# One of four gated one-hots built by two ScalarE activations instead of one VectorE instruction

## The chip, the cores and the metric

The kernel runs as one program on one core of a Trainium2 chip. A core has a matrix engine (TensorE, "PE" in the profile, with its weight loads as "PEld"), three engines for elementwise work (VectorE "DVE", ScalarE "ACT", GpSimd "POOL") and a queue engine that issues most transfers (SyncE "SP"). The metric is the device time of one execution in microseconds (us). Every engine takes its own instructions in a fixed order and waits at semaphores for the others.

## The reference, cut to what matters

The reference is a two-block transformer on 512 tokens of width 1024. The change lies in its last part, a mixture with 16,384 experts whose index is a pair (ia, ib) of 128 by 128:

```python
def _peer(h, w_q, sub_keys_1, sub_keys_2, expert_u, expert_v):
    ...
    best, ci = lax.top_k(cand, PEER_TOPK)
    ia = jnp.take_along_axis(i1, ci // PEER_TOPK, axis=-1)
    ib = jnp.take_along_axis(i2, ci % PEER_TOPK, axis=-1)
    expert_idx = ia * PEER_NKEYS + ib
    gates = jax.nn.softmax(best, axis=-1)
    ...
        a = jax.nn.gelu(jnp.einsum('td,thkd->thk', hx, u).astype(jnp.float32), approximate=False) * gx
        return jnp.einsum('thk,thkd->td', a.astype(hx.dtype), v)
```

Each token chooses 8 heads x 16 = 128 experts, each with a gate. Gates are softmax values, so they are not negative.

## The kernel before, in words

For 384 of the 512 tokens the kernel does not gather the chosen experts. It computes the activation of all experts for all 384 tokens, and multiplies by a dense table of gates that is zero where an expert was not chosen. (The other 128 tokens gather their experts' rows later.) This makes three stages of `phase_c` (line 1008 on):

1. Scores, top-16 choices, and 19 blocks of expert activations ahead (`pull(8 * 19)`).
2. **The gate stage**, which the change touches (lines 1087 to 1130). A column of 128 partitions holds the 128 choices of one token. For each token, `o1` is the one-hot of `ia` along 128 columns, `o2` is the one-hot of `ib` times the gate, and one product of the two sums the 128 choices into the token's 128 x 128 table of gates. Four tokens make a group, 384 tokens make 96 groups, 8 groups make a chunk `c` of 32 tokens, and there are 12 chunks.
3. The weighted sum over experts: per block `j` of 128 experts the table times the activations, then three matmuls per output tile (lines 1254 to 1256).

`T` holds the transposed `ia`, `ib` and gate of 128 tokens (line 1099, a ScalarE copy out of PSUM), so that one token's value is one column, a number for each partition. `one_hots(g)` makes the operands of group `g`: one VectorE comparison of 512 columns for `o1` (line 1107), and for `o2` four instructions of 128 columns (line 1112), `iota == ib` times gate: three on VectorE, and `u = 3` on GpSimd. `o1` and `o2` have three buffers each, so the one-hots of a group can be written when the matmuls of the third group before it have read theirs.

TensorE's order is written by hand: the four products of group `g` (line 1125, each is recorded as two matmuls), then one step of the next expert block (`pull(1)`, line 1081, three matmuls at lines 85 to 87). Eight steps make a block: its weights `wr` come by a SyncE transfer, ScalarE rounds them into `wh` (line 79, 128 x 1024), GpSimd takes the remainder `wl` (line 81), and after the eighth step ScalarE applies Gelu into `a` (line 1036). After each group ScalarE copies the 512 columns of the product from PSUM into `gb` with a stride (line 1128), and after each chunk it issues the transfer of `gb` to memory (line 1130). VectorE, ScalarE, GpSimd and SyncE have their orders from a scheduler in this stage; instructions wait in that order.

After the last group 16 further steps stand on TensorE, and the first `w`, `wh` and `wl` of stage 3 are made; SyncE loads the gate table back (`G`) and the first expert rows (`vr`).

Of the kernel before, what the change touches and what calls it, by code (L numbers as in the profile page):

```python
# [9 lines left out]
F32 = mybir.dt.float32  # L10
# [3 lines left out]
AF = mybir.ActivationFunctionType  # L14
# [11 lines left out]
TD = 384  # L26
NE = 16384
NA = 28
POOL_U = (3,)
POOL_A = True  # L30
LAG = 20
ZB, RT = (0, 1, 7), (1.5, 1.1)
# [13 lines left out]
class Build:  # L46
# [538 lines left out]
    def phase_b(self):  # L585
# [16 lines left out]
        with tc.tile_pool(name="pg", bufs=1, reuse_waits="tile") as pg:  # L602
# [134 lines left out]
            def decays(h):  # L737
                q, k = qk[2 * h], qk[2 * h + 1]
                T = 1.0 / 16
                b6, b12 = self.s2(name="b64"), self.s2(name="b128")  # L740
# [7 lines left out]
                dec = pg.tile([128, 4], F32, name="dec", tag="dec", bufs=2)  # L748
                for t, src, sc, by, e in ((qd, b6, T, q, nc.vector), (ki, b6, -T, k, nc.vector),
                                          (k2, d12, T, k, nc.gpsimd), (ke, d6, T, k, nc.gpsimd),  # L750
                                          (q2, b12, T, q, nc.vector)):
                    nc.scalar.activation(t, src, AF.Exp, scale=sc)
# [255 lines left out]
    def phase_c(self, x3):  # L1008
        nc, i, tc, pc = self.nc, self.i, self.tc, self.pc
# [6 lines left out]
        iota = pc.tile([128, 128], F32, name="iota")  # L1016
# [22 lines left out]
        with tc.tile_pool(name="p1", bufs=1, reuse_waits="tile") as p1:  # L1039
# [22 lines left out]
            for tt in range(4):  # L1062
                t = p1.tile([128, 1024], F32, name="x3t", tag="S_", bufs=3)
                for hf in range(2):
                    ps = self.bank()
# [19 lines left out]
        def pull(n):  # L1085
            for _ in range(n):
                next(al, None)
                self.pulled += 1

        with tc.tile_pool(name="p2", bufs=1, reuse_waits="tile") as p2:  # L1090
            ia, ib, gt = self.choose(0, NT, vals, idxs, p2)
            pull(8 * 19)
            Ts = []
            for tt in range(NT):
                ps = self.bank()
                for n, t in enumerate((ia, ib, gt)):
                    nc.tensor.transpose(ps[:, 128 * n:128 * n + 128], t[:, tt], self.ident)
                T = p2.tile([128, 3, 128], F32, name="T", tag="T", bufs=3)
                nc.scalar.activation(T, ps[:, :384].rearrange("p (n t) -> p n t", t=128), AF.Copy)
                Ts.append(T)  # L1100

            def one_hots(g):

                T, t0 = Ts[g // 32], 4 * (g % 32)
                o1 = p2.tile([128, 4, 128], F32, name="o1", tag="o1", bufs=3)
                o2 = p2.tile([128, 4, 128], F32, name="o2", tag="o2", bufs=3)
                nc.vector.tensor_tensor(o1, iota[:, None, :].to_broadcast([128, 4, 128]),
                                        T[:, 0, t0:t0 + 4].unsqueeze(2).to_broadcast([128, 4, 128]),
                                        op=OP.is_equal)
                for u in range(4):  # L1110
                    e = nc.gpsimd if u in POOL_U else nc.vector
                    e.tensor_scalar(o2[:, u], iota, T[:, 1, t0 + u:t0 + u + 1], T[:, 2, t0 + u:t0 + u + 1],
                                    op0=OP.is_equal, op1=OP.mult)
                return o1, o2

            oh = {0: one_hots(0)}
            for c in range(TD // 32):
                gb = self.xp.tile([128, 128, 32], F32, name="gb", tag="X")
                for g in range(8 * c, 8 * c + 8):
                    if g + 1 < TD // 4:  # L1120
                        oh[g + 1] = one_hots(g + 1)
                    o1, o2 = oh.pop(g)
                    ps = self.bank()
                    for u in range(4):
                        nc.tensor.matmul(ps[:, 128 * u:128 * u + 128], o1[:, u], o2[:, u], start=True, stop=True)
                    pull(1)
                    gs = 4 * (g % 8)
                    nc.scalar.activation(gb[:, :, gs:gs + 4].rearrange("p j t -> p t j"),
                                         ps.rearrange("p (t j) -> p t j", j=128), AF.Copy)
                nc.scalar.dma_start(out=gd[c], in_=gb)  # L1130
            spx = self.xp.tile([128, 4, 1024], F32, name="spx", tag="X")
            h2t, ysp, rep, fg = [spx[:, n] for n in range(4)]

            n = TD // 32 - 1
            G = {0: spx[:, 2:].rearrange("p n d -> p (n d)")[:, :4 * TD].rearrange("p (c t) -> p c t", t=128)}
            nc.sync.dma_start(out=G[0][:, :n], in_=gd[:n, :, :4].rearrange("c p j t -> p c (j t)"))
            nc.scalar.activation(G[0][:, n], gb[:, :4].rearrange("p j t -> p (j t)"), AF.Copy)
            pull(8)
# [3 lines left out]
        for hf in range(2):  # L1142
            ps = self.bank()
# [6 lines left out]
        with tc.tile_pool(name="p3", bufs=1, reuse_waits="tile") as p3:  # L1150
# [88 lines left out]
            for j in range(NJ):  # L1239
# [34 lines left out]
                if j == last + 2:  # L1274
                    assert es == 256 and not got
                    for hf in range(2):
                        ps = self.bank()
# [193 lines left out]
```

## Time and profile before

| what | value |
|---|---|
| median of 3 runs | 2256.93 us (2253.89 to 2257.43) |
| the profiled execution | 2257.13 us, of which the span is 2255.3 us |
| PE busy | 2131.9 us, 95% |
| DVE, ACT, POOL busy | 75%, 42%, 38% |
| gate stage, first group to last copy | 1098.3 to 1252.2 us |

The span runs from the first to the last recorded instruction; 1.8 us of the execution lie outside it. A share of busy time is a mean over stages with different limits, so the rows further below are taken from the gate stage and from the places where the same kinds of instruction occur elsewhere.

### The profile page before, as it was taken

To read this page: it belongs to the slowest core of one execution; us is meant where nothing else is said; L and a number is where in the kernel's file an instruction comes from. 1 tells how busy PE (TensorE), PEld (TensorE's weight loads), DVE (VectorE), ACT (ScalarE), POOL (GpSimd) and SP (SyncE) were. 2 spreads that over 40 slices of the span, in tenths; PEclk is the share of its full clock that TensorE was granted. 3 is DMA by queue.
4 is the path that set the end of the run, shared out by engine and by line. 5 is a ranking of instruction groups with operands and counts; after the bars stand their busy time and mean duration, and the time that the engine had idled before them with its cause. 6 is when DMAs were issued, how large, how long until landed. Compare 5 with 4: busy or idle time off the path is not lost. (4 is left out here: it accounts for less than half of the span.)

```text
span 2255.3 us, 31436 instructions
## 1 busy us (share of the span) xinstructions
PE 2131.9 (95%) x11443; PEld 1877.8 (83%) x11443; DVE 1692.6 (75%) x3304; ACT 958.5 (42%) x1429; POOL 847.9 (38%) x630
## 2 busy tenths in 40 slices
PE   8999999989999999999699889999999999999996
PEld 5778988877888889899688878888888888888875
DVE  6877348996667555879999678777777787877875
ACT  5376446344245533343477433333333333333332
POOL 4333330110056313335699224444444444444200
PEclk9999999999999999999899999999999999999998
DMA  6511223214822132233254659899899898899952
GB/s 249 182 48 63 79 82 112 90 57 132 274 89 66 66 107 91 93 124 120 99 202 197 227 177 333 303 322 319 307 320 312 293 319 308 309 312 309 336 184 74
DMA packets 163164, 433.08 MB, mean 192 GB/s; under 512 B 13248, under 2 KB 69952, under 8 KB 161472
## 3 DMA queue, kind: packets, MB, share of 16 engines
q1 hardware_dynamic: 121536, 267.47, 35.2%
q0 software_dynamic: 36864, 134.23, 17.2%
q10 hardware_dynamic: 4608, 29.36, 3.3%
q8 instruction: 90, 1.47, 0.3%
q14 instruction: 66, 0.54, 0.1%
HBM read 399.56 MB, written 31.46 MB: 191 GB/s over the span
## 5 line engine op out<-in xcount | busy, mean ns | idle before, releaser
L79 ACT ACTIVATE wh<-wr 128x1024 fp32r<-128x1024 f32 (+2 forms) x278 | 291.3, 1048 | 608.9 <-issue 341.0
L85 PE MATMUL bank<-h2h,wh 128*128 128x384 f32 (+2 forms) x1176 | 417.3, 355 | 22.3 <-ACT a L1036 17.5
L87 PE MATMUL bank<-h2h,wl 128*128 128x384 f32 (+2 forms) x1176 | 400.9, 341 | 4.4 <-POOL wl L81 4.4
L86 PE MATMUL bank<-h2l,wh 128*128 128x384 f32 (+2 forms) x1176 | 400.2, 340 | 0.0
L81 POOL TENSOR_TENSOR wl<-wr,wh 128x1024 fp32r<-128x1024 f32 (+2 forms) x89 | 213.9, 2407 | 414.2 <-ACT wh L79 412.0
L1255 PE MATMUL bank<-wl,wwh 128*128 128x512 f32 x768 | 302.8, 394 | 2.5 <-DVE wl L81 2.5
L1254 PE MATMUL bank<-wh,wwh 128*128 128x512 f32 x768 | 300.5, 391 | 2.3 <-ACT wwh L79 2.3
L1256 PE MATMUL bank<-wh,wwl 128*128 128x512 f32 x768 | 302.3, 394 | 0.0
L1159 POOL DMA_INDIRECT rows<-in_u_rows,sidx x128 | 176.8, 1381 | 292.4 <-DVE junk L1166 186.1
L81 DVE TENSOR_TENSOR wl<-wr,wh 128x1024 fp32r<-128x1024 f32 x189 | 233.4, 1236 | 50.5 <-ACT wh L79 49.4
L1159 POOL DMA_INDIRECT rows<-in_v,sidx x128 | 178.4, 1394 | 245.2 <-DVE spx L1176 206.0
L85 PEld LDWEIGHTS bank<-h2h,wh 128*128 128x128 f32 x1176 | 224.3, 191 | 51.8 <-ACT a L1036 43.7
L87 PEld LDWEIGHTS bank<-h2h,wl 128*128 128x128 f32 x1176 | 223.7, 190 | 9.4 <-POOL wl L81 5.3
L86 PEld LDWEIGHTS bank<-h2l,wh 128*128 128x128 f32 x1176 | 224.5, 191 | 4.9
L81 DVE TENSOR_TENSOR wwl<-w,wwh 128x384 fp32r<-128x384 f32 x128 | 71.5, 559 | 162.5 <-ACT wwh L79 162.5
L1255 PEld LDWEIGHTS bank<-wl,wwh 128*128 128x128 f32 x768 | 145.1, 189 | 32.3 <-DVE wl L81 3.7
L1254 PEld LDWEIGHTS bank<-wh,wwh 128*128 128x128 f32 x768 | 145.2, 189 | 31.1 <-ACT wwh L79 2.7
L1256 PEld LDWEIGHTS bank<-wh,wwl 128*128 128x128 f32 x768 | 145.2, 189 | 30.5
L1176 DVE SCALAR_TENSOR_TENSOR spx<-rows,coef,spx 128x1024 f32<-128x1024 f32 x127 | 162.9, 1282 | 2.5
L81 DVE TENSOR_TENSOR wl<-vr,wh 128x1024 fp32r<-128x1024 f32 x112 | 137.1, 1224 | 35.5 <-ACT wh L79 35.5
L85 PE MATMUL bank<-hh,wh 128*128 128x512 f32 (+1 forms) x408 | 160.6, 394 | 1.2 <-ACT rel L626 0.7
L1166 DVE SCALAR_TENSOR_TENSOR junk<-rows,spx 128x1024 bf16<-128x1024 f32 x128 | 156.5, 1223 | 2.8
(433 smaller groups left out, 4573.2 us busy)
## 6 DMA issues: line engine op xcount, KB each, us to landing
wr<-in_u SPq DMA_DIRECT2D x128, 512.0 KB, 5.8
vr<-in_v SPq DMA_DIRECT2D x112, 512.0 KB, 5.1
wada<-in_w_adaT SPq DMA_DIRECT2D x48, 512.0 KB, 4.3
wr<-in_w_b SPq DMA_DIRECT2D x48, 512.0 KB, 3.5
gates_d<-gb ACTq DMA_DIRECT2D x12, 2048.0 KB, 6.9
G<-gates_d SPq DMA_DIRECT2D x31, 768.0 KB, 9.5
wr<-in_w_q SPq DMA_DIRECT2D x16, 512.0 KB, 3.5
wr<-in_v SPq DMA_DIRECT2D x16, 512.0 KB, 5.3
```

The lines of the kernel that those rows point to most:

```text
L79: nc.scalar.activation(hi, src, AF.Copy)
L81: e.tensor_tensor(lo, src, hi.bitcast(F32), op=OP.subtract)
L85: mm(ps, wh, ah, start=first, stop=False)
L86: mm(ps, wh, al, start=False, stop=False)
L87: mm(ps, wl, ah, start=False, stop=last)
L1159: nc.gpsimd.indirect_dma_start(out=r, out_offset=None, in_=table, in_offset=bass.IndirectOffsetOnAxis(ap=ix, axis=0))
L1166: nc.vector.scalar_tensor_tensor(junk, r, 1.0, h2t, op0=OP.mult, op1=OP.mult, accum_out=asp[:, e:e + 1])
L1176: nc.vector.scalar_tensor_tensor(ysp, r, coef[:, e:e + 1], ysp, op0=OP.mult, op1=OP.add)
L1254: nc.tensor.matmul(y, wh[:, ts_], vh[:, ns], start=(jj == 0), stop=False)
L1255: nc.tensor.matmul(y, wh[:, ts_], vl[:, ns], start=False, stop=False)
L1256: nc.tensor.matmul(y, wl[:, ts_], vh[:, ns], start=False, stop=(jj == NJ - 1))
```

## The change

`T` gets a fourth column block, the negated gate, by one more ScalarE copy for each of the three `T`. In `one_hots`, token `u = 1` of a group is no longer made by VectorE but by ScalarE in two steps: the square of `ib - iota`, and then the positive part of `gate - gate * square` in place. The square is 0 at the chosen column and at least 1 elsewhere, so the result is the gate at that column and 0 elsewhere. The second step waits for the first by a semaphore of ScalarE itself.

```diff
-POOL_U = (3,)
+POOL_U, ACT_U = (3,), (1,)
...
-                T = p2.tile([128, 3, 128], F32, name="T", tag="T", bufs=3)
-                nc.scalar.activation(T, ps[:, :384].rearrange("p (n t) -> p n t", t=128), AF.Copy)
+                T = p2.tile([128, 4, 128], F32, name="T", tag="T", bufs=3)
+                nc.scalar.activation(T[:, :3], ps[:, :384].rearrange("p (n t) -> p n t", t=128), AF.Copy)
+                nc.scalar.activation(T[:, 3], ps[:, 256:384], AF.Copy, scale=-1.0)
...
                 for u in range(4):
+                    if u in ACT_U:
+
+                        ib, gate, minus = [T[:, n, t0 + u:t0 + u + 1] for n in (1, 2, 3)]
+                        nc.scalar.activation(o2[:, u], iota, AF.Square, bias=ib, scale=-1.0)
+                        nc.scalar.activation(o2[:, u], o2[:, u], AF.Relu, bias=gate, scale=minus)
+                        continue
                     e = nc.gpsimd if u in POOL_U else nc.vector
```

The new lines shift the numbers: the copy into `gb` is line 1135 in the changed kernel, its transfer 1137, the square 1115 and the positive part 1116.

On ScalarE, before, a chunk in the middle of the gate stage is eight copies into `gb`, one rounding `wh`, one Gelu `a` and one transfer:

```order
L1128 ACTIVATE gb_10728<-bank_10736 128x4x128
L1128 ACTIVATE gb_10728<-bank_10755 128x4x128
L1128 ACTIVATE gb_10728<-bank_10771 128x4x128
L1128 ACTIVATE gb_10728<-bank_10793 128x4x128
L1128 ACTIVATE gb_10728<-bank_10809 128x4x128
L1128 ACTIVATE gb_10728<-bank_10825 128x4x128
L1128 ACTIVATE gb_10728<-bank_10841 128x4x128
L79 ACTIVATE wh_10920<-wr_10918 128x1024
L1128 ACTIVATE gb_10728<-bank_10857 128x4x128
L1036 ACTIVATE a_10880<-bank_10743 128x384
L1130 DMA gates_d_8407<-gb_10728 128x4096
```

Now each copy has a square and a positive part beside it; this is the middle of the same chunk:

```order
L1115 ACTIVATE o2_10787<-iota_8411,T_10429 128x128
L1115 ACTIVATE o2_10810<-iota_8411,T_10429 128x128
L1116 ACTIVATE o2_10787<-o2_10787,T_10429 128x128
L1116 ACTIVATE o2_10810<-o2_10810,T_10429 128x128
L1135 ACTIVATE gb_10748<-bank_10794 128x4x128
L1115 ACTIVATE o2_10827<-iota_8411,T_10429 128x128
L79 ACTIVATE wh_10951<-wr_10949 128x1024
L1116 ACTIVATE o2_10827<-o2_10827,T_10429 128x128
L1135 ACTIVATE gb_10748<-bank_10817 128x4x128
L1115 ACTIVATE o2_10844<-iota_8411,T_10429 128x128
L1116 ACTIVATE o2_10844<-o2_10844,T_10429 128x128
L1135 ACTIVATE gb_10748<-bank_10834 128x4x128
```

In the stage's 96 groups there are now 288 instructions for what were 96; in 48 groups the positive part stands right behind the square that it waits for, as in the last group shown, and in 48 another instruction stands between. The number of activation-table loads in the whole program is 32 in both kernels.

On SyncE, at the end of the gate stage, this is the order before (`spx` takes the first gates, `vr` the first expert rows of stage 3, `wr` the weights of a further block):

```order
L1136 DMA spx<-gates_d 128x11x128
L1196 DMA vr<-in_v 128x1024 x2
L91 DMA wr<-in_u 128x1024
L1184 DMA G<-gates_d 128x12x128 x2
L1196 DMA vr<-in_v 128x1024 x2
```

And now:

```order
L1143 DMA spx<-gates_d 128x11x128
L91 DMA wr<-in_u 128x1024
L1203 DMA vr<-in_v 128x1024 x2
L1191 DMA G<-gates_d 128x12x128 x2
L1203 DMA vr<-in_v 128x1024 x2
```

The two loads of `vr` have moved behind the load of `wr`. TensorE's order is the same in both.

## Rows read from the trace of the kernel before

**Rows 1.** Busy time by engine in the gate stage (windows: us, then engines, clock, DMA)
```profile
1097.00:1110.00 13.00, 12.71 (x81) 12.31 (x80) 12.70 (x37) 8.23 (x11) 12.42 (x9) 0.79 0.00 0
...
1098.50:1252.30 153.80, 141.26 (x1061) 138.41 (x1062) 151.71 (x382) 114.57 (x119) 150.79 (x106) 0.99 0.51 194
...
1150.00:1170.00 20.00, 17.07 (x132) 16.50 (x131) 20.00 (x48) 13.70 (x14) 20.00 (x14) 1.00 0.62 237
```
**Rows 2.** Groups by form, 1097 to 1252 us: busy us, mean ns, idle before
```profile
L1112 DVE TENSOR_SCALAR o<-iota,T 128x128 f32<-128x128 f32 x288 | 107.9, 428 | 0.0
...
L1128 ACT ACTIVATE gb<-bank 128x512 f32<-128x512 f32 x96 | 103.3, 1095 | 39.2 <-PE bank L1125 38.0
...
L79 ACT ACTIVATE wh<-wr 128x1024 fp32r<-128x1024 f32 x11 | 11.7, 1066 | 0.0
L1036 ACT ACTIVATE a<-bank 128x384 f32<-128x384 f32 x11 | 5.9, 533 | 0.0
```
**Rows 3.** Waits in the gate stage: total us, times, longest
```profile
ACT gb L1128 <- PE bank L1125: 38.0, 67, 2.3
...
PE bank L1125 <- DVE o L1112: 10.2, 8, 1.7
```
**Rows 4.** Timeline of PE, two groups that follow each other: start, us, instruction
```profile
1182.06 1.05 PE L1125 MATMUL bank<-o,o 128*128 128x128 f32 x8
...
1183.48 0.72 PE L1125 MATMUL bank<-o,o 128*128 128x128 f32 x5
```
**Rows 5.** Timeline of POOL, DVE and PE around one stall
```profile
1189.06 2.87 POOL L81 TENSOR_TENSOR wl<-wr,wh 128x1024 fp32r<-128x1024 f32 x1
...
1189.62 2.90 DVE L1112 TENSOR_SCALAR o<-iota,T 128x128 f32<-128x128 f32 x3
...
1193.04 0.92 DVE L1112 TENSOR_SCALAR o<-iota,T 128x128 f32<-128x128 f32 x3
...
1192.15 1.15 PE L1125 MATMUL bank<-o,o 128*128 128x128 f32 x8 [1.43 <-DVE o L1112]
```
**Rows 6.** Timeline of ACT where it does not wait
```profile
1185.45 1.06 ACT L79 ACTIVATE wh<-wr 128x1024 fp32r<-128x1024 f32 x1
1186.40 1.09 ACT L1128 ACTIVATE gb<-bank 128x512 f32<-128x512 f32 x1
1187.27 0.54 ACT L1036 ACTIVATE a<-bank 128x384 f32<-128x384 f32 x1
...
1187.95 2.02 ACT L1128 ACTIVATE gb<-bank 128x512 f32<-128x512 f32 x2
```
**Rows 7.** Groups of ACT by form, whole span
```profile
L537 ACT ACTIVATE hh<-tmp,ada 128x256 fp32r<-128x256 f32 x16 | 7.0, 498 | 7.6 <-DVE tmp L535 7.6
...
L496 ACT ACTIVATE qb<-x,fe 128x256 f32<-128x256 f32 x6 | 3.0, 508 | 7.0 <-DVE x L494 4.1 <-DVE hl L538 1.6 <-POOL qb L138 1.3
...
L497 ACT ACTIVATE qa<-x 128x256 f32<-128x256 f32 x6 | 2.4, 401 | 0.0
...
L1137 ACT ACTIVATE spx<-gb 128x128 f32<-128x128 f32 x1 | 0.3, 300 | 0.0
```
**Rows 8.** Timeline of ACT, an activation that reads the one before it
```profile
395.61 0.62 ACT L752 ACTIVATE q<-b 128x512 f32<-128x512 f32 x1
396.26 0.21 ACT L754 ACTIVATE dec<-q 128x4 f32<-128x4 f32 x1
```
**Rows 9.** Timeline of ACT, first groups of the stage
```profile
1100.41 1.09 ACT L1128 ACTIVATE gb<-bank 128x512 f32<-128x512 f32 x1 [1.49 <-PE bank L1125]
1102.88 1.09 ACT L1128 ACTIVATE gb<-bank 128x512 f32<-128x512 f32 x1 [1.38 <-PE bank L1125]
```
**Rows 10.** Timeline of SP and ACT at the end of the stage
```profile
1246.44 1.16 SPq L1196 DMA_DIRECT2D vr<-in_v  x2
1255.58 0.33 SPq L91 DMA_DIRECT2D wr<-in_u  x1
...
1258.82 2.00 ACT L79 ACTIVATE wh<-vr 128x1024 fp32r<-128x1024 f32 x2
```

## The prediction

> **What bounds the kernel now.** The change touches only the gate stage, so I read that stage and not the page's shares. First the busy time by engine in the stage's 153.8 us [rows 1]: DVE and POOL are recorded as busy nearly all of it, PE for 141.3 and ACT for 114.6. That looks like a stage bound by VectorE, with ScalarE having room. The reader is to check this look in two ways.
>
> The first is the pace of PE. Two undisturbed groups start 1.42 us apart (1182.06 and 1183.48) [rows 4], and no wait of PE falls there. So between stalls PE is the bound: 96 groups at 1.42 us are 136.3 us. The rest of the stage, 17.5 us, is the slow start and a stall of about 1.5 us in eight chunks. In such a stall [rows 5] POOL does a remainder `wl` of 2.87 us, DVE's three one-hots take 2.90 us instead of 0.92, and PE then sits idle for 1.43 us until DVE's `o` comes; there are 8 such waits, 10.2 us together [rows 3]. This is all that a faster VectorE can give back.
>
> The second is what ScalarE really has free. The sum of recorded durations misleads, because neighbours overlap in the records. Where ACT does not wait [rows 6], a copy into `gb` begins at 1186.40 and the next instruction at 1187.27: it holds the engine for about 0.88 us, not the 1.09 recorded. A `wh` holds it 0.95 us (1185.45 to 1186.40), and Gelu with the transfer issue behind it 0.68 (1187.27 to 1187.95). By the counts in [rows 2] ScalarE holds 96 x 0.88 + 11 x 0.95 + 11 x 0.68 = 84.5 + 10.5 + 7.5 = 102.5 us of the stage's 153.8. So 51 us are free, most of it as waits for PE's product (38.0 us, 67 times [rows 3]). Per group that is 0.53 us.
>
> **What the change removes.** On VectorE 96 of 288 instructions of 128 columns; three take 0.92 us [rows 5], so a group loses 0.31 us. VectorE then has slack before PE, and with three buffers the stall of [rows 5] is mostly covered. On its own this would be worth up to the stalls.
>
> **What it adds on ScalarE.** 96 squares and 96 positive parts. No such instruction with 128 columns and these operands stands in the trace of before, so I build it from neighbours. A plain 128-column activation from SBUF to SBUF takes 300 ns [rows 7]. An operand that is a column of numbers costs about 0.1 us: 256 columns with a column as scale 508 ns, with a column as bias 498, with neither 401 [rows 7]. So a square (bias a column) records 0.395 us. The positive part has two columns, bias and scale; the second may cost nothing (0.395) or the same again (0.49). I take 0.49, since a column costs the same in either place and there is no row in which one is free. Neighbours that don't depend on each other overlap by 0.1 us (`wh`, 1.06 long, and its successor 0.95 later [rows 6]); an activation that reads the one before starts 0.03 us after its end (395.61 + 0.62, then 396.26 [rows 8]). So:
>
> - a square with something else behind it: 0.30 us, 48 of them: 14.4
> - a square with its own positive part right behind it, which waits for its end: 0.425 us, 48 of them: 20.4
> - a positive part: 0.395 us (0.30 if the second column is free), 96 of them: 37.9 (28.8)
>
> Together 72.7 us (63.6) against 51.3 free. ScalarE becomes the bound, and the stage grows by 72.7 - 51.3 = 21.4 us (12.3). If ScalarE had no such self-wait and a free second column, 96 x 0.60 = 57.6 would leave +6.3; if no neighbour overlapped, 96 x (0.395 + 0.49) + 1.5 for the self-waits = 86.5 would make it +35.2. These are the ends of the range for this term.
>
> The Trainium skill, "ScalarE: Activation LUTs", section "What ACT_TABLE_LOAD costs", gives an activation 186 ns plus 0.833 ns per column, about 93 ns more for each pointer operand, and 93 ns of overlap. The rows agree to a few ns for none and one pointer (293 against 300 ns, +93 against +97 and +107); no row has two. By that rule the positive part holds the engine 0.39 us and the stage grows by 20 us; by a free second operand it would be 12.3.
>
> Does ScalarE keep busy, or does it also wait? In its new order a group's one-hot is made about two copies ahead of that group's own copy, so PE has some 2 us to follow before ScalarE asks for its product. What stands behind a waiting positive part is the next copy, `wh` for GpSimd and PE, Gelu and the gate transfer; all become later together, so nothing beyond the stage's own growth is charged. The negated gates, three small copies, fall in part into the gaps between the `T` copies: 0.4 us. At the start PE is granted 0.79 on average, so part of the stretch to 1110 us is at the lower level of 1.2 GHz [rows 1]; the first two copies are 2.47 us apart, each after a wait of 1.4 us [rows 9]; there ScalarE can't work at its own pace, about 1 us more.
>
> **What moves.** SyncE now puts the two `vr` loads behind the `wr` load. Before, they were issued at 1246.44, `wr` at 1255.58, and `wh` was taken from `vr` at 1258.82 [rows 10]. So the `vr` loads had 12 us before they were needed; behind `wr`, which waits for GpSimd's remainder to free its buffer, they keep about 3. I charge 0 to 3 us and take 1. TensorE's order is unchanged.
>
> Sum against the profiled execution: 2257.1 + 21.4 + 1.4 + 1 = 2280.9, **2281 us**, 24 us or 1.1% slower. The median of the runs, 2256.93, differs from that execution by 0.2 us, so the same number holds for it.
>
> **Rivals.**
>
> *A, faster: VectorE was the limit and ScalarE has room.* For it: DVE is busy for 151.7 of 153.8 us, and all eight stalls end at DVE's `o`. The Trainium skill, "Perfetto Trace Analysis", section "Optimizing Scalar/DVE Operations", says that where DVE is saturated, moving work to Scalar may pay; DVE's busy time in this stage agrees with the condition. The place is PE's stalls, the price is theirs: PE alone would need 136.3 us, plus 2.5 for the half-clock start, 139 instead of 153.8, so the time would be 2257 - 15 = 2242 us. It decides at 0.38 us a group: if a square and a positive part hold ScalarE less than (139 - 102.5) / 96 each group, PE stays the bound. Against it: two activations of 300 ns can't do so without overlapping by half. Chance 5%.
>
> *B, within 0.2%: cheap activations and a hand-back.* The two at 0.60 us per group give +6; if in addition the end of the stage hands a few us back (after it PE waits for expert rows and gates that come by transfer), the result is 2257 to 2262, say 2260. Against it: the self-wait of [rows 8] costs in half of the groups, and a free column is in no row. Chance 7%.
>
> *C, much slower: PE's clock.* A bound by ScalarE leaves PE about 1.37 us of work in groups of 1.83. In [rows 1] PE kept the granted clock at 1.00 with 17.07 of 20 us busy, but there the idle time lies in a few stalls and not in every group. Under the lower level the first groups were 2.47 us apart [rows 9], 0.64 more than 1.83; if a third of the groups ran so, 32 x 0.64 = 20 us more, 2301. Chance 9%.
>
> That the change does not do what it says is excluded by its order: 192 activations are there, and no more table loads than before.
>
> **How the numbers follow.** My forecast (ScalarE bound, 2264 to 2296 by the ends of the ScalarE term with the smaller ones) has 79%, with 2281 as its point. The range 2263 to 2298 leaves out A and B (12%) and about 7% of C and the tail. About 0.2%, or 4.5 us, is what a measurement of this kernel can tell from no change. Faster than that: A, and a bit of B, 6%. Within: the rest of B, 6%. Slower: 88%.
>
> **What would show it.** In the gate stage of the changed kernel: the stage 22 us longer; ACT without waits for PE's product between the first and the last chunk; positive part 0.49 us, square 0.40; PE idle in each group, ended by ScalarE's `o`; DVE and POOL with waits, and the eight 1.4 us stalls gone or hidden; clock 1.00. After it: `wh` from `vr` no more than 3 us late. I am wrong in the mechanism if ACT still waits 30 us or more for PE; wrong in a size if a positive part takes 0.40 us, or if a copy into `gb` holds the engine other than 0.88 us when a square follows it.

## The result: 0.9% slower, and ScalarE sets the pace of the gate stage

The changed kernel takes 2276.59 us (median of 4 runs, 2275.53 to 2277.86), against 2256.36 us for the kernel before (4 runs). The ratio is 1.0091, with an interval of 1.0074 to 1.0109. The profiled execution took 2275.53 us, 18.4 us longer than the one before.

I measure the gate stage from PE's first product to the end of the last copy into `gb`. Before it lasted 153.9 us (1098.30 to 1252.22), now 173.0 us (1095.38 to 1268.36): 19.1 us longer. It also begins 2.9 us earlier, in phases that the change does not touch. After the stage nothing changes at first: from the last copy to the first product of stage 3, 9.35 us pass in both traces. From there to the end it is 996.1 us against 993.8. So 19.1 - 2.9 + 2.3 = 18.5 us, the difference of the spans. The gate stage holds all of the loss.

First the windows of the changed kernel, with the columns of [rows 1]: the whole stage, and 20 us from its middle.

```profile
1095.38:1268.36 172.98, 150.55 (x1061) 142.18 (x1062) 136.45 (x286) 167.05 (x312) 141.94 (x107) 0.99 0.44 174
1150.00:1170.00 20.00, 17.04 (x124) 16.32 (x125) 16.77 (x38) 19.27 (x38) 17.71 (x15) 1.00 0.42 158
```

In the middle of the stage DVE has gone from 20.00 busy us of 20 to 16.77 and POOL from 20.00 to 17.71, while ACT has gone from 13.70 to 19.27. The granted clock stayed at 1.00. VectorE was relieved as meant, and ScalarE is full.

The groups of ACT and POOL in the stage, with busy time, mean duration, and idle time before them, show the prices.

```profile
L1135 ACT ACTIVATE gb<-bank 128x512 f32<-128x512 f32 x96 | 103.0, 1075 | 1.9 <-PE bank L1132 1.9
L1116 ACT ACTIVATE o<-o,T 128x128 f32<-128x128 f32 x96 | 45.8, 491 | 1.6
L1115 ACT ACTIVATE o<-iota,T 128x128 f32<-128x128 f32 x96 | 34.7, 376 | 0.0
...
L1036 ACT ACTIVATE a<-bank 128x384 f32<-128x384 f32 x11 | 5.4, 491 | 2.5 <-PE bank L1132 2.2 <-ACT o L1115 0.2
...
L81 POOL TENSOR_TENSOR wl<-wr,wh 128x1024 fp32r<-128x1024 f32 x11 | 31.2, 2835 | 20.3 <-ACT wh L79 20.3
```

A positive part is recorded with 491 ns and a square with 376. Before, the copies into `gb` had 39.2 idle us in front of them [rows 2]; now 1.9 are left. The waits of the stage say who is late instead (who waited for what: total us, times, longest).

```profile
DVE o L1108 <- PE bank L1132: 32.9, 73, 1.8
POOL wl L81 <- ACT wh L79: 20.3, 11, 1.9
...
PE bank L1132 <- POOL o L1119: 11.2, 11, 1.0
PE bank L1132 <- ACT o L1116: 10.1, 12, 1.4
...
ACT gb L1135 <- PE bank L1132: 1.9, 4, 0.7
```

Before, ScalarE waited for PE 67 times and PE for VectorE's `o` 8 times [rows 3]. Now PE waits for two things: about once a chunk for ScalarE's `o`, and about once a chunk for GpSimd's. GpSimd's `wl` waits 20.3 us for ScalarE's `wh`.

How long an instruction holds ScalarE is read from the starts of neighbours. Here is ACT's timeline over one `wh` and two whole groups (start, us, instruction).

```profile
1189.06 1.09 ACT L79 ACTIVATE wh<-wr 128x1024 fp32r<-128x1024 f32 x1
1190.00 0.53 ACT L1116 ACTIVATE o<-o,T 128x128 f32<-128x128 f32 x1
1190.39 1.11 ACT L1135 ACTIVATE gb<-bank 128x512 f32<-128x512 f32 x1
1191.24 0.41 ACT L1115 ACTIVATE o<-iota,T 128x128 f32<-128x128 f32 x1
1191.68 0.49 ACT L1116 ACTIVATE o<-o,T 128x128 f32<-128x128 f32 x1
1192.08 1.04 ACT L1135 ACTIVATE gb<-bank 128x512 f32<-128x512 f32 x1
1192.93 0.36 ACT L1115 ACTIVATE o<-iota,T 128x128 f32<-128x128 f32 x1
1193.32 0.49 ACT L1116 ACTIVATE o<-o,T 128x128 f32<-128x128 f32 x1
1193.72 1.07 ACT L1135 ACTIVATE gb<-bank 128x512 f32<-128x512 f32 x1
```

From copy to copy it is 1193.72 - 1192.08 = 1.64 us: the copy holds the engine 0.85, the square with its self-wait (the time until its own positive part may start) 0.39, the positive part 0.40. No wait for another engine is shown. Where something else stands behind the square a group is shorter, and the mean of all 96 is 1.60 us (33.6 + 37.3 + 82.8 us, in a table further below). At the end of a chunk Gelu follows:

```profile
1183.84 0.33 ACTq L1137 DMA_DIRECT2D gates_d<-gb  x1
1184.21 0.49 ACT L1036 ACTIVATE a<-bank 128x384 f32<-128x384 f32 x1 [0.25 <-PE bank L1132]
1184.60 1.04 ACT L1135 ACTIVATE gb<-bank 128x512 f32<-128x512 f32 x1
```

Gelu holds the engine 0.39 us. The 0.25 us of idle time ahead of it are put down to PE, but the last product that goes into what Gelu reads had ended at 1183.47. What fills this time is the issue of the gate transfer, 0.33 us from 1183.84 on. So eight groups, one `wh` (0.94), one Gelu and the issue ahead of it make 12.8 + 0.94 + 0.39 + 0.25 = 14.4 us for a chunk. Twelve chunks make 173 us, which is the stage: ScalarE is the bound.

The last fence shows where PE pays it, in the same chunk: POOL, DVE and PE.

```profile
1190.23 2.83 POOL L81 TENSOR_TENSOR wl<-wr,wh 128x1024 fp32r<-128x1024 f32 x1 [1.86 <-ACT wh L79]
...
1190.74 2.66 DVE L1119 TENSOR_SCALAR o<-iota,T 128x128 f32<-128x128 f32 x2
...
1185.95 0.94 PE L1132 MATMUL bank<-o,o 128*128 128x128 f32 x6 [0.85 <-ACT o L1116]
...
1193.95 0.49 PE L1132 MATMUL bank<-o,o 128*128 128x128 f32 x2 [1.01 <-POOL o L1119]
```

DVE's two one-hots beside `wl` still take 2.66 us instead of 0.60, as the three did in [rows 5], but now they end in time. PE waits for GpSimd's own one-hot, which stands behind `wl`.

### The profile page after: what moved, and what is told of

Its sections match the earlier page's. It is cut to its first block, busy times and chain, and to the rows that moved or that the text cites. A ratio compares the mean times of both kernels' runs of the same rounds, so it can differ in the third digit from the quotient of the medians.

```text
span 2273.8 us, 31602 instructions
## 1 busy us (share of the span) xinstructions
PE 2140.8 (94%) x11443; PEld 1881.7 (83%) x11443; DVE 1673.8 (74%) x3208; ACT 1010.2 (44%) x1624; POOL 836.4 (37%) x630
## 5 line engine op out<-in xcount | busy, mean ns | idle before, releaser
L1036 ACT ACTIVATE a<-bank 128x384 f32<-128x384 f32 x128 | 62.6, 489 | 218.4 <-DVE w L1194 213.1
```

Of the source, the lines that this page charges most:

```text
L1036: nc.scalar.activation(a, ps[:, :TD], AF.Gelu)
```

## The experiments

The ratios are against the kernel before on the same chip, whose median beside the runs below the second row was 2255.56 to 2255.68 us. "Stage" and "idle" are read as above, from the profiled execution; of the 5.9 us of the change 1.6 are self-waits, 2.5 the transfer's issue and 1.9 waits ahead of copies.

| kernel | median us | ratio (interval) | stage us | ACT idle in it |
|---|---|---|---|---|
| before | 2256.36 | 1 | 153.9 | 39.2 |
| the change | 2276.59 | 1.0091 (1.0074 to 1.0109) | 173.0 | 5.9 |
| relief_alone | 2242.84 | 0.9951 (0.9937 to 0.9966) | 140.0 | 25.1 |
| square_only | 2247.50 | 0.9968 (0.9957 to 0.9979) | 140.9 | 10.4 |
| one_column | 2268.53 | 1.0064 (1.0047 to 1.0080) | 164.6 | 5.7 |
| early_square | 2273.93 | 1.0089 (1.0073 to 1.0106) | 167.1 | 3.2 |
| flat_after | 2258.80 | 1.0018 (1.0008 to 1.0028) | 157.9 | 20.1 |
| wl_on_vector | 2270.01 | 1.0068 (1.0052 to 1.0085) | 171.9 | 6.4 |
| flat_and_wl | 2238.50 | 0.9927 (0.9909 to 0.9945) | 140.5 | 7.5 |
| half_dose | 2253.67 | 0.9994 (0.9985 to 1.0004) | 150.6 | 9.6 |
| half_earlier | 2251.24 | 0.9979 (0.9970 to 0.9988) | 145.6 | 10.3 |
| three_of_eight | 2249.96 | 0.9978 (0.9969 to 0.9987) | 147.0 | 17.2 |

What lies outside the stage varies between kernels by some us (2098 to 2107 when the stage is taken from the median), so a step of a few us is read from the stage, and the median only confirms the larger ones.

**relief_alone: VectorE's relief without ScalarE's work.**

```diff
-                for u in range(4):
-                    if u in ACT_U:
...
+                for u in (0, 2, 3):
...
-                        nc.tensor.matmul(ps[:, 128 * u:128 * u + 128], o1[:, u], o2[:, u], start=True, stop=True)
+                        nc.tensor.matmul(ps[:, 128 * u:128 * u + 128], o1[:, u], o2[:, 0 if u == 1 else u], start=True, stop=True)
```

> The kernel before with two instead of three VectorE one-hots per group and nothing added on ScalarE; the product of token u = 1 reads the one-hot of u = 0, so one token in four gets a wrong table, with the same work on TensorE. It measures what the removed VectorE work is worth. If VectorE's lateness is the cause of the eight stalls, the stage falls towards TensorE's 139 us: 2242 to 2246 us. If the stalls are GpSimd's own (its u = 3 stands behind the 2.87 us remainder wl, whatever VectorE does), the stage stays near 153 us: 2253 to 2257.

```profile
ACT gb L1128 <- PE bank L1125: 23.9, 66, 1.6
...
PE bank L1125 <- DVE o L1112: 1.3, 2, 1.0
```

The stage is 140.0 us, 13.9 shorter than before, and PE's eight waits for VectorE (10.2 us [rows 3]) have shrunk to two with 1.3 us. PE starts a group every 1.42 us and ScalarE waits for it again. So the relief is real and worth what PE's pace allows. It was taken back by what ScalarE was given: 140.0 to 173.0 us.

**square_only: occupancy or latency?** The positive part is left out, the square stays.

```diff
                         nc.scalar.activation(o2[:, u], iota, AF.Square, bias=ib, scale=-1.0)
-                        nc.scalar.activation(o2[:, u], o2[:, u], AF.Relu, bias=gate, scale=minus)
```

> The changed kernel without the positive part (the square is used as it is, so the gates of u = 1 are wrong). Theory 1, ScalarE's occupancy sets the stage: 102.5 + 96 x 0.28 = 129 us of work on ScalarE is under TensorE's 139, so the result equals the relief alone, 2242 to 2247 us. Theory 2, each group waits for the way through ScalarE's queue (latency, not occupancy): the wait stays with the first activation, and about half of the loss remains, 2262 to 2268 us.

```profile
1098.45:1239.31 140.86, 140.86 (x1061) 139.14 (x1062) 132.46 (x286) 130.45 (x216) 136.42 (x107) 0.98 0.52 205
```

A one-hot that still comes from ScalarE, with half of its work, costs nothing: the stage is at PE's pace (PE busy 140.86 of 140.86 us). That the operand comes from another engine is not what costs; the time for which ScalarE is held is.

**one_column: the price of the second column.** The positive part loses its bias column.

```diff
-                        nc.scalar.activation(o2[:, u], o2[:, u], AF.Relu, bias=gate, scale=minus)
+                        nc.scalar.activation(o2[:, u], o2[:, u], AF.Relu, scale=minus)
```

> The changed kernel with the positive part without its bias column (the gate is not added, so u = 1 gives zeros); it reads one column operand instead of two. It measures the second column, which no row of the kernel before had. Theory 1, occupancy: 0.095 us less for each of 96, all of it in the time, 9 us less: 2266 to 2269 us. If the second column is free: 2275 to 2277 us. If GpSimd's stalls set the stage beside ScalarE: 2270 to 2275 us.

```profile
L1116 ACT ACTIVATE o<-o,T 128x128 f32<-128x128 f32 x96 | 37.0, 399 | 1.9
```

The recorded duration falls from 491 to 399 ns, and the stage by 8.4 us; 96 x 0.092 = 8.8. So the second column costs the same again, and on a full ScalarE it reaches the stage nearly whole. The Trainium skill, "ScalarE: Activation LUTs", section "What ACT_TABLE_LOAD costs", puts about 93 ns on each pointer operand; this run agrees for the second.

**early_square: the self-wait.** The square of the next group goes into a tile of its own, ahead of this group's positive part, so that no positive part stands right behind its own square.

```diff
+            def square(g):
+                if g < TD // 4:
+                    T, t1 = Ts[g // 32], 4 * (g % 32) + 1
+                    squares[g] = p2.tile([128, 128], F32, name="sq2", tag="sq2", bufs=3)
+                    nc.scalar.activation(squares[g], iota, AF.Square, bias=T[:, 1, t1:t1 + 1], scale=-1.0)
...
+                square(g + 1)
...
+                        nc.scalar.activation(o2[:, u], squares.pop(g), AF.Relu, bias=gate, scale=minus)
```

> The changed kernel with the square of the next group issued before the positive part of this one, into a tile of its own; no positive part stands right behind its own square any more (48 did). Nothing is left out. Theory 1, occupancy: 48 self-waits of about 0.12 us go, 5 to 6 us less, 2270 to 2273 us. Theory 2, latency of the way through ScalarE: the squares are ahead by a whole group, so more than that goes, under 2268 us. If the self-wait costs nothing: 2276.

```profile
1285.00 1.06 ACT L79 ACTIVATE wh<-vr 128x1024 fp32r<-128x1024 f32 x1 [10.07 <-DMA vr<-in_v]
...
1286.49 0.69 PE L85 MATMUL bank<-h2h,wh 128*128 128x384 f32 x1 [10.10 <-ACT a L1036]
```

By the starts of neighbours the 96 squares with their self-waits held ScalarE 33.6 us in the changed kernel and hold it 28.0 here, and the stage is 5.9 us shorter. The median falls by 2.7 us only, and the intervals of the ratios overlap. From the first product of stage 3 on, the run is 3.2 us longer than the changed kernel: there `wh` waits 10.07 us for the second pair of `vr`, against 7.50, and PE stands idle for 10.10 us, against 6.69. So the self-wait is shown in the stage; as a gain of the kernel it is not settled.

**flat_after: the copy without its stride.** The group's 512 columns are written to `gb` side by side, where the change writes the 128 values of each token 32 columns apart.

```diff
-                    nc.scalar.activation(gb[:, :, gs:gs + 4].rearrange("p j t -> p t j"),
-                                         ps.rearrange("p (t j) -> p t j", j=128), AF.Copy)
+                    nc.scalar.activation(gb[:, 4 * gs:4 * gs + 16], ps.rearrange("p (j t) -> p j t", t=32), AF.Copy)
```

> The changed kernel with the copy of each group's product written without a stride (same 512 columns, other places, so the gate table is permuted). A 512-column copy without stride records 0.60 us and would hold ScalarE about 0.5 instead of 0.88 us. Theory 1, occupancy: 96 x 0.38 = 36 us less on ScalarE, 175 becomes 139, TensorE is the bound again: 2242 to 2248 us. Theory 2, latency of the one-hots: they are not touched, 2270 to 2277 us.

```profile
ACT gb L1135 <- PE bank L1132: 14.0, 25, 1.4
...
PE bank L1132 <- POOL o L1119: 11.8, 10, 1.2
```

```profile
1187.11 9.97 POOL L1119 TENSOR_SCALAR o<-iota,T 128x128 f32<-128x128 f32 x8
1197.05 2.92 POOL L81 TENSOR_TENSOR wl<-wr,wh 128x1024 fp32r<-128x1024 f32 x1
```

The copy is recorded with 589 ns instead of 1075 and holds the engine 0.48 to 0.49 us instead of 0.86. ScalarE waits again, and the stage is 157.9 us: 15 better than the change, but 18 worse than relief_alone. This fell between what the theories had led me to expect, and the wait says why: PE now stands once a chunk for GpSimd's `o`, and for nothing else that repeats. There is a second limit behind ScalarE's. It is what GpSimd has to do: from 1123 to 1238 us it is recorded without idle time, and eight one-hots and one `wl` make 9.97 + 2.92 = 12.9 us, which is the chunk of this run (seven groups of 1.42 us and one of 2.92).

**wl_on_vector and flat_and_wl: the second limit alone, and both.** VectorE takes the `wl` from GpSimd, ten of the eleven that the stage holds, with the strided copy and with the flat one (`gating` is true during the stage).

```diff
-                    au[j + 1] = self.wload(i["u"][j + 1], [8, 128], True)
+                    au[j + 1] = self.wload(i["u"][j + 1], [8, 128], not gating)
```

> The changed kernel with the 11 remainders wl of the gate stage computed by VectorE (which waits 33 us there) in place of GpSimd. Nothing is left out. Theory 1, ScalarE's occupancy sets the stage: the 1.5 us stall of TensorE behind GpSimd's wl in each chunk goes, but ScalarE has the same work, so the time hardly changes, 2271 to 2277 us. Theory 3, the stage of the changed kernel is the sum of its stalls and GpSimd's remainder is one cause beside ScalarE: 11 x 1.5 = 16 us come back, 2258 to 2264 us.

> The run flat_after (copy without a stride, gate table permuted) with the remainders wl on VectorE as well. flat_after left a stall of 1.5 us in each chunk, ended by GpSimd's one-hot, and ScalarE idle for 20 us. If GpSimd's wl is the cause of what kept flat_after at 2258.8, both limits are gone and TensorE's pace remains: 2241 to 2247 us. If the cause is ScalarE's waiting chain after all: 2255 to 2260 us.

```profile
1093.67:1265.56 171.89, 151.91 (x1061) 142.11 (x1062) 124.15 (x296) 165.52 (x309) 128.44 (x97) 0.99 0.46 180
```

```profile
1095.13:1235.60 140.47, 139.33 (x1058) 138.00 (x1059) 121.26 (x297) 132.92 (x311) 123.74 (x97) 0.99 0.55 215
```

The first window is that of wl_on_vector, the second that of flat_and_wl. PE's waits in wl_on_vector:

```profile
PE bank L1134 <- ACT o L1118: 14.6, 11, 1.4
...
PE bank L1134 <- DVE o L1121: 4.5, 11, 1.2
```

The four stages stand in a square:

| stage us | `wl` on GpSimd | `wl` on VectorE |
|---|---|---|
| strided copy | 173.0 (the change) | 171.9 |
| flat copy | 157.9 | 140.5 |

Taking `wl` away alone gives 1.1 us, although PE waited 11.2 us for what stands behind it. In place of that wait PE waits longer for ScalarE's `o` (14.6 us against 10.1) and now for VectorE's, behind the `wl` that it has taken over (4.5 us against 0.3). Once ScalarE is light, the same step gives 17.4. So the two waits that looked alike in the list of waits are a bound (ScalarE's) and a symptom (GpSimd's) that becomes the bound later. The median of wl_on_vector is 6.6 us below the change's; 5.5 of these lie outside the stage and are not explained. flat_and_wl took 2238.50 us, a little less than expected. Its stage is at PE's pace like that of relief_alone (140.5 and 140.0 us), so this difference too lies outside the stage and is not explained.

**half_dose: ScalarE's one-hot in every second group.**

```diff
-                    if u in ACT_U:
+                    if u in ACT_U and g % 2:
```

> ScalarE builds the one-hot of u = 1 in every second group only; in the others VectorE has three, as before. Nothing is left out. Theory 1, occupancy: 102.5 + 48 x 0.75 = 138 us on ScalarE is about TensorE's 139, VectorE still gets half of its relief, so the stage is near TensorE's pace: 2243 to 2250 us, faster than both kernels. If the loss went by the number of one-hots on ScalarE (latency of each), half of it remains: 2264 to 2268 us. If GpSimd's remainder keeps one stall in each chunk: 2255 to 2260 us.

ACT, and then PE, around one stall:

```profile
1175.62 1.06 ACT L79 ACTIVATE wh<-wr 128x1024 fp32r<-128x1024 f32 x1
...
1178.74 0.39 ACT L1115 ACTIVATE o<-iota,T 128x128 f32<-128x128 f32 x1
1179.00 1.05 ACT L1135 ACTIVATE gb<-bank 128x512 f32<-128x512 f32 x1
1179.83 0.49 ACT L1116 ACTIVATE o<-o,T 128x128 f32<-128x128 f32 x1
...
1180.37 0.94 PE L1132 MATMUL bank<-o,o 128*128 128x128 f32 x6 [0.90 <-ACT o L1116]
```

The stage is 150.6 us and the time the kernel's before, within the interval. That is more than the 2243 to 2250 us expected from occupancy. ScalarE has about as much work in a chunk as PE (14.4 - 4 x 0.74 = 11.4 us against 8 x 1.42 = 11.4), but once a chunk `wh`, Gelu and the copies stand in front, a copy stands between square and positive part, and PE waits 0.9 us. That ScalarE's order costs here is what the next two runs test.

**half_earlier and three_of_eight: the same, asked for earlier.** The two activations get a higher priority in the scheduler; three_of_eight has them in three groups of eight (`g % 8 in (1, 5, 7)`).

```diff
+                        with self.tc.high_priority(offset=20):
+                            nc.scalar.activation(o2[:, u], iota, AF.Square, bias=ib, scale=-1.0)
+                            nc.scalar.activation(o2[:, u], o2[:, u], AF.Relu, bias=gate, scale=minus)
```

> half_dose with a higher priority for the two activations in the scheduler, so that on ScalarE each positive part stands before the copy of two groups earlier, also behind wh and Gelu, where it stood one copy later in half_dose (its group was the one at which TensorE stalled 1.1 us in each chunk). Same work, nothing left out. If that place in the queue is the cause of half_dose's stall, 11 x 1.1 = 12 us come back less what ScalarE lacks: 2241 to 2248 us, faster than both kernels. If the stall only moves to another group, because 138 us on ScalarE leave no slack: 2251 to 2257 us.

> As half_earlier, with ScalarE building u = 1 in three groups of eight (the second, sixth and eighth of a chunk). ScalarE has 102.5 + 36 x 0.75 = 130 us, 9 us under TensorE's pace. Nothing is left out. With that slack and the early place there is no stall from ScalarE; VectorE is relieved in 36 groups: 2242 to 2248 us. If VectorE's relief is too small and the old stalls behind GpSimd's wl return: 2250 to 2256 us.

```profile
ACT o L1116 <- PE bank L1133: 7.8, 20, 0.9
...
PE bank L1133 <- DVE o L1120: 4.6, 11, 0.5
```

These are waits of half_earlier; its window from 1150 to 1200 us is this:

```profile
1150.00:1200.00 50.00, 48.28 (x371) 47.13 (x369) 50.00 (x118) 47.06 (x77) 50.00 (x39) 1.00 0.58 228
```

PE no longer waits for ScalarE's `o`, so it was ScalarE's order that cost in half_dose. What is left is a wait for VectorE beside `wl`, 4.6 us in all: VectorE and GpSimd are busy for 50.00 of 50 us. The stage is 145.6 us and the time 2251.24, ratio 0.9979 (0.9970 to 0.9988). Neither run reached the range I had given for a stall that goes away (2241 to 2248 and 2242 to 2248 us). half_earlier lies in the one for a stall that only moves, and three_of_eight at the lower end of its own; in both the stall has moved to VectorE (4.6 and 7.1 us). Both versions are faster than both kernels, by little; between the two nothing can be told (the intervals overlap). Of the 13.9 us that the relief offers in the stage they keep 8.3 and 6.9.

## Why the prediction was right, and where it was not

The forecast was 2281 us, in the direction and by the mechanism that came: ScalarE becomes the bound. The stage was to grow by 22.8 us (21.4 and 1.4) and grew by 19.1; the rest of the miss is that it began 2.9 us earlier, which nothing in the forecast or in the change accounts for, less 1.3 us behind the stage.

| term, 96 groups | predicted us | measured us |
|---|---|---|
| squares, half of them with the self-wait behind them | 14.4 + 20.4 = 34.8 | 33.6 |
| positive parts | 37.9 | 37.3 |
| copies into `gb` | 84.5 | 82.8 |
| `wh` | 10.5 | 10.4 |
| Gelu and the transfer's issue | 7.5 | 4.2 + 2.5 = 6.7 |
| idle time of ScalarE ahead of copies | about 1 | 1.9 |

The measured column adds up the distances between the starts of neighbours, without idle time but for the self-waits (the 1.6 us ahead of the positive parts in the groups above) and the 2.5 us ahead of Gelu, in which the transfer is issued.

- *What is free on ScalarE*: right, and the step on which all else stands. Neither the recorded 1.09 us of a copy nor the 39 idle us, but the distance of starts gave the 51 us that were set against the 72.7 of new work.
- *The copy*: the largest error of size in the sum, 1.7 us. The rows shown give 0.87 us (1187.27 - 1186.40) where 0.88 was taken; 0.86 were measured.
- *PE the bound between the stalls of the kernel before*: right for single groups, not for a chunk. From one stalled set of VectorE's one-hots to the next 13.0 us pass (1176.60 to 1189.62), which is the chunk, and VectorE and GpSimd have no idle time in it; PE's eight groups alone need 11.4. So the first look, a stage that is not PE's, held for these chunks. Which of the two engines sets the pace there is not separated: without the third one-hot on VectorE (relief_alone) GpSimd's eight fall from 10.21 to 8.56 us as well. The price did not depend on it: relief_alone gave 13.9 us back. The window of the kernel before from 1150 to 1200 us:

```profile
1150.00:1200.00 50.00, 44.23 (x339) 43.08 (x338) 50.00 (x123) 36.45 (x38) 50.00 (x35) 1.00 0.52 201
```

- *The second column*: 0.49 us predicted, 491 ns recorded, and one_column shows it in the stage.
- *The square*: 0.395 us predicted, 376 ns recorded. The 48 squares with their positive part right behind them are recorded with 368 ns, and 0.033 us pass before the positive part starts: 0.401 us in place of 0.425. The other 48 hold the engine 0.299 us; 0.30 was predicted.
- *Gelu with the transfer*: 0.68 us was read from a place where the next copy followed the transfer's issue [rows 6]. In the changed kernel the issue stands ahead of Gelu and begins while the square before it still runs. Gelu holds the engine 0.39 us, about 0.22 us are idle ahead of it, and 0.8 us fewer are used in all.
- *A slip that nothing rests on*: of the growths of 20 and 12.3 us given side by side, 12.3 is the sum from the rows (63.6 - 51.3); by the rule that gives 20 it would be about 11.
- *The handoff*: 1 us was charged for the `vr` loads behind `wr`. There is none at first: the loads land in time, as the rows below show. The second pair of `vr` does come later, and `wh` waits 7.50 us for it (6.2 before). There 1.25 of the +2.3 us arise; the rest comes in steps of less than 0.4 us up to the end and is not explained.

SP, then ACT, at the end of the stage, to be held against [rows 10]:

```profile
1264.42 0.34 SPq L91 DMA_DIRECT2D wr<-in_u  x1
1264.85 0.86 SPq L1203 DMA_DIRECT2D vr<-in_v  x2
...
1273.28 1.05 ACT L79 ACTIVATE wh<-vr 128x1024 fp32r<-128x1024 f32 x1
...
1287.19 1.06 ACT L79 ACTIVATE wh<-vr 128x1024 fp32r<-128x1024 f32 x1 [7.50 <-DMA vr<-in_v]
```

- *"PE idle in each group, ended by ScalarE's `o`"*: wrong in shape. PE runs four to six groups of a chunk at 1.42 us and pays in two places: a pair of groups of 2.5 and 1.8 us for ScalarE's `o`, and one of 2.9 us for GpSimd's. With three buffers of `o2` ScalarE gets ahead during the one wait and is caught up before the next: in the chunk shown its positive part ends 1.2 us ahead of the product that reads it behind GpSimd's wait, and 0.05 us ahead at the pair.
- *"The eight 1.4 us stalls gone or hidden"*: wrong. The stalls stay and change their releaser, from VectorE's to GpSimd's `o`. I had looked only at who waits behind `wl` on VectorE, and not at what stands behind it on GpSimd, nor that `wl` itself would wait 1.86 us for a later `wh`. It cost the prediction nothing, since ScalarE's sum is larger; with a lighter ScalarE it would have cost 17 us, as the square of four stages shows.
- *Rival A* put 2242 us on a kernel in which the relief costs ScalarE nothing; relief_alone took 2242.84. *Rival C* did not come: the granted clock was 1.00, the upper level of 2.4 GHz, in the middle of the stage with PE busy for 17.04 of 20 us.

What stays open: why GpSimd keeps up in one kernel and not in another. In relief_alone its eight one-hots between two `wl` take 8.56 us, in flat_after 9.97. The first three are alike (0.85, 0.97 and 1.13 us); the last five take 1.13 to 1.18 us each in relief_alone, and 1.41 in flat_after:

```profile
1146.88 8.56 POOL L1112 TENSOR_SCALAR o<-iota,T 128x128 f32<-128x128 f32 x8
```

```profile
1177.17 7.06 POOL L1119 TENSOR_SCALAR o<-iota,T 128x128 f32<-128x128 f32 x5
1184.21 2.92 POOL L81 TENSOR_TENSOR wl<-wr,wh 128x1024 fp32r<-128x1024 f32 x1
```

The first is relief_alone, the second flat_after with its last five. In flat_after each of these starts within 0.05 us of one of VectorE's comparisons of 512 columns; in relief_alone a one-hot starts 0.3 us after one. The Trainium skill, "SBUF — State Buffer", section "Who interferes with whom", has VectorE instructions with two SBUF inputs contend with GpSimd's reads, which would fit; a run that separates the two starts was not made.

## What to carry to other kernels

Before an engine is given work, add up what it has free by the distance between the starts of its neighbouring instructions, per period of the loop, and compare the new sum with the period of the engine that sets the pace: here 14.4 us for a chunk against 11.4. Look at what stands ahead of an idle time before taking it for a wait: the issue of a transfer is not counted as busy. Then look at what the engine that is moved past has behind it, since the next limit (GpSimd's `wl`, and what stands behind it) shows only when the first is gone. A part of the move (three or four groups of eight), asked for early enough, kept 4.4 and 5.7 us of the 12.7 by which relief_alone's median is shorter, where the whole move lost 20.

## What the runs showed of the hardware

- A ScalarE copy of 512 columns out of PSUM that writes its values 32 columns apart holds the engine 0.86 us; written side by side it holds it 0.49 us, and is recorded with 589 instead of 1075 ns. It was the largest price on the busiest engine, larger than the two new activations together (0.74), and I had not looked at it as one that could be had for less.
- A self-wait on ScalarE costs little by itself, 0.033 us, but it takes away the overlap: a square with its own positive part behind it keeps the engine 0.401 us from start to start, one with other work behind it 0.299, and 0.292 in early_square.
